# Moving the prompt's two key and value tiles behind the attention's first scores, and reloading weights in quarter pieces

## The chip, the cores and the metric

The kernel runs on one core of a Trainium2 chip. Its time is the device time of one execution in microseconds (us). Before the change the median of three runs is 1297.93 us (1297.85 to 1300.37).

## What is computed

The reference is one step of a two-layer backbone over 256 context ("prompt") tokens and 1024 latent ("sample") tokens of width 1024. Layer 0 is gated linear attention, layer 1 grouped-query softmax attention with 8 query heads and 2 key/value heads of size 128. The change lies in layer 1, at the seam between the output of layer 0 and the attention:

```
qp, kp, vp, gp = attn_project(hp, att_w_in, qnorm, knorm)      # prompt tokens
out_p = (attend_blocks(qp, kp, vp) * silu(gp)) @ att_w_out
ctx_keys.append(kp); ctx_vals.append(vp)                       # also outputs of the kernel
qs, ks_, vs, gs = attn_project(hs, att_w_in, qnorm, knorm)     # sample tokens
keys = concatenate([rope_2d(ks_), cache_k]); vals = concatenate([vs, cache_v])
out_s = (attend_blocks(rope_2d(qs), keys, vals) * silu(gs)) @ att_w_out
```

A sample query reads 1280 keys: the 1024 sample ones and 256 from a cache. Only the prompt's own queries read the prompt's keys and values.

## The kernel before

Every float32 product is made of three float16 ones: each factor is split into a high and a low part, and `mm3` (line 123) adds high by high, high by low and low by high. So one projection of 128 tokens to 512 columns is 24 matmuls of 512 columns, and one key and value tile, which reads its weights as two blocks of 256 columns (`pieces`, line 511), is 48 matmuls of 256 columns.

The tokens are cut into ten tiles of 128: 0 and 1 are the prompt, 2 to 9 the sample. `gla_out` (line 822) ends layer 0: it adds the residual, normalises, transposes, and makes the key and value tiles of all ten (`key_tile`, line 998), the sample's first and the prompt's last, by `keys(0)` on its last line, after the first two query projections. A key tile is a projection into a PSUM bank (tag "kv"), a copy to the tile `hx` on ScalarE (ACT), a norm of each head, a split of key and value into high and low, and a transposing DMA of the key into `kT` from the queue of SyncE (SP). For a prompt tile, ACT also writes the value into the only buffer of the tag "rope" (line 1012) and sends key and value to HBM.

`attention` (line 1141) then goes through ten steps, each a pair of a key head and a chunk of 256 tokens, four query heads to a step. The order of chunks is 1, 2, 3, 4, 0 for the first key head and 1, 0, 2, 3, 4 for the second; chunk 0 is the prompt, so steps 4 and 6 (counted from 0) are the prompt's. One head takes, for each of its two halves of 128 queries:

- `scores` (line 1043): 9 matmuls into S (three PSUM banks, two buffers), a maximum on VectorE (DVE, line 1059), an exponential on ACT (line 1064);
- `rest` (line 1070), held back by one half: the reciprocal, the division and split (line 1085 on GpSimd, POOL; line 1086 on DVE), and the transposing DMA to `PT` (line 1087, SP queue);
- two heads later `values` (line 1098): 30 matmuls on PT (6 for a prompt chunk).

Between the scores, `query` and `query_rest` make queries some steps ahead, and after each second head `gateT` (line 1090) makes two gates. The weights of these come from HBM: `load_w` (line 1113) calls `wload` (line 235), which with a list `later` puts its transfers there, and `attention` issues one from the list at each head. The query weights of the second key head ("q1") are listed at step 0, the gate weights ("g1") at step 4, the output weights ("o0") at step 6. Each lands in one of three places of SBUF; q1's place is the one that holds the first half of the key weights until the key tiles have read them.

The order written here is only a priority. A planner simulates the program when it is built and places each engine's instructions as soon as it believes them ready, so that a transfer can be issued well ahead of its line. On the chip each engine and each DMA queue then keeps the planned order.

Of the kernel before, what the change touches and what calls it, by code (L numbers as in the profile page):

```python
# [8 lines left out]
F32 = mybir.dt.float32  # L9
# [8 lines left out]
P = 128  # L18
D = 1024
KT = D // P  # L20
# [7 lines left out]
HD, AH, KVH = 128, 8, 2  # L28
# [28 lines left out]
class K:  # L57
# [126 lines left out]
    def fill(self, w, j, st):  # L184
        nc = self.nc
        s, w[2][j] = self.scale(st)
        h = KT // 4
        for i in range(4):
            a, n = slice(i * h, i * h + h), slice(256 * j, 256 * j + 256)
            hi, lo = w[0][:, a, n], w[1][:, a, n]  # L190
            nc.scalar.activation(hi, st[:, a, :], AF.Copy, scale=s)
            nc.vector.scalar_tensor_tensor(lo, st[:, a, :], s, hi, ALU.mult, ALU.subtract)
# [42 lines left out]
    def wload(self, name, place, later=None):  # L235
        d, inv = self.ahead.pop(name)
        w = self.wtile(place)[0:2]
        if later is None:
            for j, t in enumerate(w):
                self.nc.sync.dma_start(t, d[:, j])  # L240
        else:
            h = KT // 2
            later += [(t[:, a : a + h], d[:, j, a : a + h]) for j, t in enumerate(w) for a in (0, h)]
        return *w, inv


# [575 lines left out]
    def gla_out(self, wo, wkv):  # L822
        nc = self.nc
        done = len(EARLY)
        xs, junk = {}, self.t(self.xp, [P, D], F16, "junk", bufs=1)
        late = list(ROWS[done:])

        def fetch(i):
            xs[i] = self.t(self.xp, [P, D], F32, "xr", bufs=6)
            nc.sync.dma_start(xs[i], xrow(self.I, i) if i in late else self.x1_d[i])  # L830

        def norm(i):
            self.normalise([xs[i], xs[i + 1]], junk)

        def turn(i):
            ys = [xs.pop(i), xs.pop(i + 1)]
            for k in range(KT):
                self.modulate(self.transpose(ys, k, "tr"), k, i)

        def out(i):  # L840
            self.row_out(i, wo, xs[i])

        def keys(i):
            for j in range(2):
                self.key_tile(i + j, wkv)

        self.gs, self.sh, self.inv_h = self.mod1
        for i in (2, 3, 8, 4, 5, 9):
            fetch(i)
        d, inv = self.ahead.pop("kv")  # L850
        for j, w in enumerate(wkv):
            for part in range(2):
                nc.sync.dma_start(w[part], d[:, part, :, 256 * j : 256 * j + 256])
        ckv = self.att_load()
        self.o1 = []
        fill = self.out_part(2, self.kept2)
        norm(2)
        out(8)
        turn(2)
        norm(4)  # L860
        fetch(6)
        fetch(7)
        out(9)
        self.att_setup(*ckv)
        self.key_setup(*ckv, inv)
        self.wq = [self.load_w("q0", 2)]
        turn(4)
        fetch(0)
        fetch(1)
        fill(0)  # L870
        keys(2)
        norm(6)
        fill(1)
        out(0)
        fill = self.out_part(3, self.kept)
        turn(6)
        norm(8)
        keys(4)
        out(1)
        self.query_start()  # L880
        turn(8)
        fill(0)
        keys(6)
        norm(0)
        self.key_tile(8, wkv)
        self.query()
        turn(0)
        fill(1)
        self.key_tile(9, wkv)
        self.query_rest()  # L890
        self.query()
        self.query_rest()
        keys(0)

# [98 lines left out]
        nc.scalar.activation(self.vh[:, 8:10, :], cv, AF.Copy, scale=sv)  # L995
        nc.vector.scalar_tensor_tensor(self.vl[:, 8:10, :], cv, sv, self.vh[:, 8:10, :], ALU.mult, ALU.subtract)

    def key_tile(self, i, w):
        nc = self.nc
        j = i - NTP if i >= NTP else 10 + i  # L1000
        ps = self.bank("kv")
        self.pieces(ps, lambda k: self.hT(k, i * P, P), w, 0, 512)
        x = self.t(self.hw, [P, 2, HD], F32, "hx")
        nc.scalar.activation(x.rearrange("p h d -> p (h d)"), ps[:, 0:256], AF.Copy, scale=self.inv_k)
        self.head_norm(x, self.kn, x)
        pv = ps[:, 256:512]
        nc.scalar.activation(self.vh[:, j, :], pv, AF.Copy, scale=self.psv)
        nc.vector.scalar_tensor_tensor(self.vl[:, j, :], pv, self.psv, self.vh[:, j, :], ALU.mult, ALU.subtract)
        if i < NTP:
            nc.scalar.dma_start(self.O[3][0, 0, i * P : i * P + P], x)  # L1010
            v = self.t(self.hw, [P, 2, HD], F32, "rope", bufs=1)
            nc.scalar.activation(v.rearrange("p h d -> p (h d)"), pv, AF.Copy, scale=self.inv_av)
            nc.scalar.dma_start(self.O[4][0, 0, i * P : i * P + P], v)
        else:
            self.rope(x, i)
        a = slice(j * P, j * P + P)
        self.split_transpose(x, self.asc[:, 1:2], self.kT[:, :, a])
# [119 lines left out]
    def query_rest(self):  # L1137
        if self.half:
            self.queries_out(self.half.pop(), 1)

    def attention(self, wo):
        self.S0, self.put_off = self.t(self.ps, [P, 1536], F32, "S"), None
        wq, wg, q, g = self.wq, self.wg, self.q, {}
        pend, later = [], []
        for n, (p, c) in enumerate(self.steps):
            if n == 0:
                wq.append(self.load_w("q1", 1, later))
            if n == 4:
                wg.append(self.load_w("g1", 2, later))
            if n == 6:  # L1150
                o0 = self.wload("o0", 0, later)
            for e in range(4):
                h = 4 * p + e
                if later:
                    self.nc.sync.dma_start(*later.pop(0))
                PT = self.t(self.sp, [P, 20, 256], F16, "PT", bufs=3)
                self.scores(h, c, 0, q[(p, c, 0)], PT)
                if e % 2 == 0:
                    self.query()
                    self.scores(h, c, 1, q[(p, c, 1)], PT)  # L1160
                else:
                    self.query_rest()
                if len(pend) == 2:
                    self.values(*pend[0], g.pop(pend.pop(0)[0]))
                if e % 2 == 1:
                    self.scores(h, c, 1, q[(p, c, 1)], PT)
                pend.append((h, c, PT))
                if e % 2 == 1:
                    g.update({i: self.gateT(i, c, *wg[p]) for i in (h - 1, h)})
                if n == 9 and e == 0:  # L1170
                    row = self.out2_load(OUT[0])
                if n == 9 and e == 1:
                    first = self.ropet.rearrange("p a b d -> p (a b d)").bitcast(F16)
                    first = first.rearrange("p (j h t) -> p j h t", j=2, h=AH)
                    with self.tc.issue_after(self.last):
                        self.prep = self.out2_prep(row, (first[:, 0], first[:, 1]))
        self.rest()
        gt = self.t(self.wst, [P, KT, 256], F32, "wst").rearrange("p (i k) n -> p i (k n)", i=2)
        self.fold_gate(1, o0[2] + [inv for _, inv in self.o1], gt)
        wo[:] = [(*o0[0:2], 512)] + [(*w, 256) for w, _ in self.o1]  # L1180
        self.out_tile(OUT[0], 0, self.t(self.sp, [P, TS + PAST], F32, "p")[:, 0:D], wo)
        for t in pend:
            self.values(*t, g.pop(t[0]))
# [289 lines left out]
def xrow(I, i):  # L1473
    if i < NTP:
        return I["x_prompt"][0, i * P : i * P + P, :]
    return I["x_sample"][0, (i - NTP) * P : (i - NTP) * P + P, :]
# [84 lines left out]
```

## Time and profile before

| | |
|---|---|
| median of 3 runs | 1297.93 us |
| profiled execution | 1297.29 us |
| its span, first to last instruction | 1295.5 us |
| TensorE (PE) matmul busy | 1212.2 us, 94% |
| VectorE busy | 898.9 us, 69% |
| ScalarE busy | 581.4 us, 45% |
| GpSimd busy | 384.2 us, 30% |
| 16 DMA engines, mean rate | 150 GB/s |

The span plus 1.8 us around it is the profiled execution's time. PE is TensorE's matmuls, and a row's length for a matmul includes the pipeline's tail, so the distance from one start to the next tells what a matmul costs. In the timeline a bracket gives the idle time of the engine before the row and what released it. PEclk is the granted clock of TensorE: 1.00 is its upper level of 2.4 GHz, 0.50 the lower one of 1.2 GHz.

### The profile page before, as it was taken

The page shows a single profiled execution, that of the slowest core. Times are in us where ns is not written, and L with a number is a line of the kernel's source. Part 1 is how long each engine was busy: PE and PEld are TensorE (multiplying, and loading weights), DVE is VectorE, ACT ScalarE, POOL GpSimd, SP SyncE. Part 2 cuts the span into 40 slices and gives each one's busy share as a digit, 9 for nine tenths or more (in the row PEclk, how much of TensorE's full clock was granted, in tenths as well). Part 3 has the DMA queues.
Part 4 walks back from the last instruction along what each step waited for, and adds up shares of the span by engine and source line. Part 5 has one row for each costly group of instructions (what it writes and reads, how often), then busy time and mean ns, then how long its engine had stood idle before and what let it go on. Part 6 is the DMA issues. An engine that isn't in the chain of part 4 may idle for free. (4 is left out here: it accounts for less than half of the span.)

```text
span 1295.5 us, 22611 instructions
## 1 busy us (share of the span) xinstructions
PE 1212.2 (94%) x8295; PEld 811.9 (63%) x8295; DVE 898.9 (69%) x2072; ACT 581.4 (45%) x1425; POOL 384.2 (30%) x617
## 2 busy tenths in 40 slices
PE   4799989999998998999899989999999999989997
PEld 2347666655555555666688756667666766767665
DVE  5545866776688988755597667877657587885652
ACT  3445555555466665411265554444445455441110
POOL 0222211322232334400044535453233345522000
PEclk9899999999999999999999999999999999999999
DMA  9511454563443434995953357767848648778542
GB/s 359 191 65 34 146 180 124 157 193 103 150 117 119 126 114 158 283 199 141 326 161 101 81 116 140 135 130 147 191 94 172 146 86 144 145 143 197 174 131 82
DMA packets 333793, 194.42 MB, mean 150 GB/s; under 512 B 229663, under 2 KB 318607, under 8 KB 332401
## 3 DMA queue, kind: packets, MB, share of 16 engines
q1 hardware_dynamic: 291616, 159.02, 49.0%
q10 hardware_dynamic: 42064, 33.95, 8.4%
q8 instruction: 65, 1.06, 0.4%
q14 instruction: 48, 0.39, 0.1%
HBM read 103.00 MB, written 33.83 MB: 106 GB/s over the span
## 5 line engine op out<-in xcount | busy, mean ns | idle before, releaser
L131 PEld LDWEIGHTS <-hT_hi 128*128 128x128 f16 x1920 | 188.0, 98 | 126.9 <-issue 14.0
L131 PE MATMUL mm<-whi,hT_hi 128*128 128x512 f16 (+1 forms) x560 | 196.5, 351 | 6.5 <-ACT gx L535 5.6
L131 PE MATMUL mm<-wlo,hT_hi 128*128 128x512 f16 (+1 forms) x560 | 196.6, 351 | 0.0
L131 PE MATMUL mm<-whi,hT_lo 128*128 128x512 f16 (+1 forms) x560 | 196.6, 351 | 0.0
L131 PEld LDWEIGHTS <-whi 128*128 128x128 f16 x1408 | 138.0, 98 | 62.1 <-issue 9.2
L131 PE MATMUL mm<-hT_hi,whi 128*128 128x256 f16 (+1 forms) x512 | 153.3, 301 | 3.6 <-POOL hT_hi L410 2.9
L1085 POOL TENSOR_SCALAR phl<-p,srec 128x1280 f16<-128x1280 f32 (+1 forms) x80 | 98.8, 1235 | 188.2 <-DVE srec L1080 105.0
L131 PE MATMUL mm<-hT_lo,whi 128*128 128x256 f16 (+1 forms) x512 | 153.6, 301 | 0.2 <-DVE hT_lo L411 0.2
L131 PE MATMUL mm<-hT_hi,wlo 128*128 128x256 f16 (+1 forms) x512 | 153.7, 301 | 0.0
L1086 DVE SCALAR_TENSOR_TENSOR phl<-p,srec,phl 128x1280 f16<-128x1280 f32 (+1 forms) x80 | 107.7, 1347 | 51.6 <-POOL phl L1085 51.3
L131 PEld LDWEIGHTS <-hT_lo 128*128 128x128 f16 x960 | 94.2, 98 | 61.7 <-issue 1.0
L1056 PE MATMUL S<-kT,wst 128*128 128x512 f16 (+1 forms) x624 | 122.9, 341 | 7.5 <-ACT p L1064 7.1
L131 PE MATMUL mm<-PT,vh 128*128 128x256 f16 x672 | 114.3, 275 | 10.9 <-DMA PT<-phl 8.5
L1064 ACT ACTIVATE p<-S,snb,sexp 128x1280 f32<-128x1280 f32 (+1 forms) x80 | 99.7, 1246 | 29.4 <-DVE phl L1086 10.2
L1059 DVE TENSOR_REDUCE smx<-S 128x1 f32<-128x1280 f32 (+1 forms) x80 | 101.6, 1270 | 15.1 <-PE S L1056 15.1
L1056 PEld LDWEIGHTS <-wst 128*128 128x128 f16 x624 | 61.4, 98 | 60.4 <-issue 10.2
L131 PE MATMUL mm<-PT,vl 128*128 128x256 f16 x336 | 92.4, 275 | 0.0
L131 PEld LDWEIGHTS <-wlo 128*128 128x128 f16 x704 | 69.0, 98 | 29.5 <-issue 1.4
L1061 ACT ACTIVATE snb<-smx,nsexp 128x1 f32<-128x1 f32 x80 | 23.4, 293 | 131.9 <-DVE smx L1059 126.6
L131 PEld LDWEIGHTS <-vh 128*128 128x128 f16 x672 | 65.8, 99 | 21.9 <-issue 10.0
L917 POOL TENSOR_TENSOR rope<-hx,ropet 128x64 f32<-128x64 f32 x160 | 69.9, 465 | 10.3 <-DVE hx L906 4.7
L153 DVE TENSOR_REDUCE wmx<-wst 128x1 f32<-128x512 f32 x96 | 59.8, 676 | 11.8 <-DMA wst<-in_gla_w_in 10.4
(347 smaller groups left out, 2494.7 us busy)
## 6 DMA issues: line engine op xcount, KB each, us to landing
wada<-in_w_ada SPq DMA_DIRECT2D x13, 1024.0 KB
wst<-in_gla_w_in SPq DMA_DIRECT2D x12, 1024.0 KB
wst<-in_att_w_in SPq DMA_DIRECT2D x10, 1024.0 KB
xr<-x_d SPq DMA_DIRECT2D x15, 512.0 KB
og_d<-qk ACTq DMA_DIRECT2D x40, 128.0 KB
wst<-og_d SPq DMA_DIRECT2D x5, 1024.0 KB
out<-xr ACTq DMA_DIRECT2D x17, 256.0 KB
x<-in_x_sample SPq DMA_DIRECT2D x8, 512.0 KB
```

Of the source, the lines that this page charges most:

```text
L131: self.nc.tensor.matmul(out, a, b, start=k == 0 and j == 0, stop=k == n - 1 and j == 2)
L153: nc.vector.tensor_reduce(mx[:, j : j + 1], st[:, 2 * j : 2 * j + 2, :], AX.XY, ALU.max, apply_absolute_value=True)
L917: nc.gpsimd.tensor_tensor(tv[:, h, :, w, :], xv[:, h, :, 1 - w, :], sn[:, :, w, :], ALU.mult)
L1056: nc.tensor.matmul(S[:, a : a + n], x, y, start=m == 0, stop=m == 2)
L1059: last = nc.vector.tensor_reduce(mx, S, AX.X, ALU.max).ins
L1061: nc.scalar.activation(nb, mx, AF.Copy, scale=self.nsexp)
L1064: nc.scalar.activation(p, S, AF.Exp, scale=self.sexp, bias=nb, accum_out=den)
L1085: nc.gpsimd.tensor_scalar(hi, p, r, 2.0 ** 14, ALU.mult, ALU.mult)
L1086: nc.vector.scalar_tensor_tensor(lo, p, r2, hi, ALU.mult, ALU.subtract)
```

## The change

The two prompt tiles leave the end of `gla_out`. Their weights are held, the second half is loaded again (its first copy lies in a pool that ends with `gla_out`) beside the first, and each tile is made in `attention` behind the first scores of heads 0 and 1 of step 0. There it uses the PSUM tag "mm" and the tile tag "hx4", both shared with the queries. The listed weight loads come as eight transfers of 256 KB in place of four of 512 KB, in order of use; q1 is listed at step 1, o0 at step 7, and g1 at step 4 from its second head on, two transfers a head, the last two at the first head of step 5.

```diff
         else:
-            h = KT // 2
-            later += [(t[:, a : a + h], d[:, j, a : a + h]) for j, t in enumerate(w) for a in (0, h)]
+            h = KT // 4
+            later += [(t[:, a : a + h], d[:, j, a : a + h]) for a in range(0, KT, h) for j, t in enumerate(w)]
...
-        keys(0)
+        self.held_keys = d, wkv
...
-    def key_tile(self, i, w):
+    def key_tile(self, i, w, tag="kv"):
...
-        ps = self.bank("kv")
+        ps = self.bank(tag)
...
-        x = self.t(self.hw, [P, 2, HD], F32, "hx")
+        x = self.t(self.hw, [P, 4, HD], F32, "hx4")[:, 0:2] if tag == "mm" else self.t(self.hw, [P, 2, HD], F32, "hx")
...
+    def prompt_keys(self):
+        d, wkv = self.held_keys
+        hi, lo, _ = wkv[0]
+        again = [t[:, :, 0:256] for t in self.nw[0:2]]
+        for part, t in enumerate(again):
+            self.nc.sync.dma_start(t, d[:, part, :, 256:512])
+        w = [wkv[0], (*again, 256)]
+        return lambda i: self.key_tile(i, w, "mm")
...
             if n == 0:
+                keys = self.prompt_keys()
+            if n == 1:
                 wq.append(self.load_w("q1", 1, later))
             if n == 4:
                 wg.append(self.load_w("g1", 2, later))
-            if n == 6:
+            if n == 7:
                 o0 = self.wload("o0", 0, later)
             for e in range(4):
                 h = 4 * p + e
-                if later:
-                    self.nc.sync.dma_start(*later.pop(0))
+                for _ in range((0, 2, 2, 2)[e] if n == 4 else 2 if n == 5 else 1):
+                    if later:
+                        self.nc.sync.dma_start(*later.pop(0))
                 PT = self.t(self.sp, [P, 20, 256], F16, "PT", bufs=3)
                 self.scores(h, c, 0, q[(p, c, 0)], PT)
+                if n == 0 and e < 2:
+                    keys(e)
```

## Rows read from the trace of the kernel before

**Rows 1.** The page, busy time and the span in 40 slices, PE and its clock.
```profile
PE 1212.2 (94%) x8295; PEld 811.9 (63%) x8295; DVE 898.9 (69%) x2072; ACT 581.4 (45%) x1425; POOL 384.2 (30%) x617
...
PE   4799989999998998999899989999999999989997
...
PEclk9899999999999999999999999999999999999999
```

**Rows 2.** Timeline of PE at the seam: start, duration, work, idle before and releaser.
```profile
729.79 0.27 PE L131 MATMUL kv<-whi,hT_hi 128*128 128x256 f16 x1
...
740.73 1.79 PE L1056 MATMUL S<-kT,wst 128*128 128x512 f16 x9
742.35 0.38 PE L131 MATMUL mm<-whi,hT_hi 128*128 128x512 f16 x1
...
747.32 0.38 PE L131 MATMUL mm<-whi,hT_lo 128*128 128x512 f16 x1
748.08 1.78 PE L1056 MATMUL S<-kT,wst 128*128 128x512 f16 x9 [0.39 <-ACT rope L1012]
753.28 3.15 PE L1056 MATMUL S<-kT,wst 128*128 128x512 f16 x9 [3.42 <-ACT p L1064]
756.27 0.27 PE L131 MATMUL mm<-hT_hi,whi 128*128 128x256 f16 x1
```

**Rows 3.** Timeline of ACT and DVE, the first softmax and what stands before it.
```profile
747.56 0.47 ACT L1012 ACTIVATE rope<-kv,inv_av 128x256 f32<-128x256 f32 x1 [2.51 <-DMA out<-rope]
749.48 0.48 DVE L934 SCALAR_TENSOR_TENSOR xhl<-hx,asc,xhl 128x256 f16<-128x256 f32 x1 [2.80 <-ACT xhl L933]
749.88 1.48 DVE L1059 TENSOR_REDUCE smx<-S 128x1 f32<-128x1280 f32 x1
751.73 1.42 ACT L1064 ACTIVATE p<-S,snb,sexp 128x1280 f32<-128x1280 f32 x1
```

**Rows 4.** Timeline of SP's queue: the last transposes and q1's four transfers.
```profile
732.33 1.19 SPq L935 DMA_TRANSPOSE kT<-xhl  x1
735.32 1.19 SPq L935 DMA_TRANSPOSE wst<-xhl  x1
736.60 1.00 SPq L1155 DMA_DIRECT2D wlo<-w_q  x2
739.64 1.20 SPq L935 DMA_TRANSPOSE wst<-xhl  x1
740.94 1.00 SPq L1155 DMA_DIRECT2D whi<-w_q  x2
```

**Rows 5.** Busy us by engine (instructions), PE clock, DMA share, GB/s, in stretches of 1 us.
```profile
734.00:735.00 1.00, 1.00 (x11) 0.80 (x10) 1.00 (x5) 0.72 (x4) 0.29 (x1) 1.00 0.16 32
735.00:736.00 1.00, 1.00 (x11) 0.90 (x10) 0.86 (x4) 0.39 (x2) 0.84 (x2) 1.00 0.00 0
740.00:741.00 1.00, 1.00 (x11) 0.80 (x9) 0.86 (x3) 0.06 (x1) 0.07 (x1) 1.00 0.94 360
754.00:755.00 1.00, 1.00 (x4) 0.35 (x3) 0.28 (x2) 0.94 (x6) 0.03 (x1) 0.50 0.00 0
```

**Rows 6.** Timeline of PE and ACT, the rest of step 0: waits, and its eighth exponential.
```profile
778.38 1.78 PE L1056 MATMUL S<-kT,wst 128*128 128x512 f16 x9 [1.77 <-ACT p L1064]
781.56 0.39 PE L131 MATMUL mm<-PT,vh 128*128 128x256 f16 x2 [1.40 <-DMA PT<-phl]
786.04 1.42 ACT L1064 ACTIVATE p<-S,snb,sexp 128x1280 f32<-128x1280 f32 x1 [1.14 <-DVE srec L1080]
```

**Rows 7.** Timeline of SP's queue and of PE, step 4 (prompt chunk) and g1's transfers.
```profile
917.24 1.01 SPq L1155 DMA_DIRECT2D whi<-w_g  x2
926.08 1.04 SPq L1155 DMA_DIRECT2D wlo<-w_g  x2
...
936.68 0.38 PE L131 MATMUL mm<-PT,vh 128*128 128x256 f16 x2
939.96 0.71 PE L1056 MATMUL S<-kT,wst 128*128 128x256 f16 x5
943.35 0.38 PE L131 MATMUL mm<-PT,vh 128*128 128x256 f16 x2 [2.69 <-DMA PT<-phl]
948.29 0.27 PE L1056 MATMUL S<-kT,wst 128*128 128x256 f16 x1
```

**Rows 8.** Busy us by engine, clock, DMA share: g1's load, then two full stretches.
```profile
925.00:930.00 5.00, 5.00 (x47) 4.33 (x45) 3.69 (x6) 2.17 (x4) 1.33 (x1) 1.00 0.97 226
930.00:935.00 5.00, 5.00 (x33) 2.94 (x31) 2.50 (x9) 1.61 (x5) 0.00 (x0) 1.00 1.16 224
800.00:850.00 50.00, 50.00 (x360) 35.05 (x359) 38.89 (x71) 23.32 (x55) 25.89 (x31) 1.00 0.68 127
```

**Rows 9.** Timeline of PE: the other wait that a load may touch, and o0's first use.
```profile
1000.20 0.38 PE L131 MATMUL mm<-PT,vh 128*128 128x256 f16 x2 [1.82 <-DMA PT<-phl]
...
1172.74 0.38 PE L131 MATMUL S<-whi,ropet 128*128 128x512 f16 x1
```

## The prediction

> **What bounds the kernel now.** I read the page first: PE is busy for 94% of the span, and apart from the first slices every slice is nearly full and the clock is at its upper level [rows 1]. No engine other than PE comes near. So the time falls only where PE stands or runs at the lower clock, and moved work gains only where it fills such a place. Next I listed PE's waits from the seam between the layers to the end of the attention; they sit at the seam and in the rest of step 0, in the prompt steps, and late in the second key head, where the change does nothing. Between, in the stretch from 800 to 850 us, PE is busy for all 50.00 us [rows 8].
>
> At the seam PE works without a gap until 747.5 us: the two prompt tiles from 729.79 to 740.73 us, the first S, a query of 24 matmuls, then a second S after 0.39 us. The third S needs a free buffer, that is the first S's exponential, and PE stands for 3.42 us [rows 2]. Why is that exponential late? The first S is complete at about 742.5 us, but its maximum starts only at 749.88 us. DVE and ACT hold the second prompt tile ahead of it: ACT's copy at 747.56 us had idled 2.51 us for the output DMA that still read the one "rope" buffer, and DVE idled 2.80 us behind ACT [rows 3]. The clock follows: after the wait it is granted at 0.50, the level of 1.2 GHz [rows 5], and the nine matmuls of the third S take 2.99 us from start to next start (753.28 to 756.27) where the first took 1.62 us (740.73 to 742.35) [rows 2].
>
> **The change, part by part.**
>
> *The prompt tiles move.* Nothing leaves PE: 96 matmuls of 256 columns before and after. They ran for 10.94 us (729.79 to 740.73, a few transposes among them) ahead of the first S [rows 2]. What did the first S wait for otherwise? The last sample key was issued to its transpose at 732.33 us [rows 4], and the DMA engines are at rest by 735 us [rows 5]. So the first S can start at about 735 us, 5.5 us earlier. PE need not stand from 730 to 735 us: the first prompt tile (half of 10.94, 5.5 us) and a query (742.35 to about 747.5, 5.2 us) are ready, and the planner may place either first. Without the prompt's vector work ahead, maximum and exponential follow at once: from the maximum's start to the exponential's end takes 3.27 us (749.88 to 751.73 plus 1.42) [rows 3]. The first buffer is then free at about 735.2 + 1.8 + 3.3 = 740.3 us. PE's way to the third S is 10.94 (tile and query, 5.5 + 5.2, rounded) + two S of 1.62 from 729.8 us, so it comes there at 743.7 us or later and finds the buffer free. The second S's 0.39 us goes with the release by the copy of line 1012, which no longer holds its bank. Gain: 0.39 + 3.42 + the lower clock's 2.99 - 1.62 = 1.37, sum 5.2 us. I take all of it; the bounds are 0 (the hold returns inside the step) and 5.2.
>
> *The rest of step 0.* The eight exponentials start 4.90 us apart on average (751.73 to 786.04, seven intervals) [rows 3, 6]. PE offers less in the first two heads: four S of 1.62, a query of 5.2, two gates of half a query each, 16.9 us or 4.2 us a half. So it catches up with the chain and stands 1.77 us for an exponential and 1.40 us for a transposed PT [rows 6]. With 10.94 us more it needs 7.0 us a half there, over 4.90, and the wait for the exponential should go: 1.8 us. The wait for PT I leave, because q1's load moves onto the first PT transposes (next part). Bounds 0 and 3.2.
>
> *The second half of the key weights is loaded again:* two transfers of 512 KB more on SP's queue. Two such issues take 1.00 us of the queue [rows 4]; at the 360 GB/s of a stretch that holds only such loads [rows 5] 1.05 MB takes 2.9 us. Lower bound 0, upper 3.9 if the planner puts them right ahead of the last key's transpose. I take 0, because PE has the 10.7 us of tile and query to do while the first S waits; without that cover the first S slips by as much.
>
> *Twelve more issues,* three loads of eight in place of four: at 0.5 us of SP's queue each [rows 4], spread one or two to a head. A transpose queued behind two waits about 1 us more; values come two heads later, over 10 us. Cost 0. If SP were already late, up to 1 us a head.
>
> *q1 moves to step 1.* It now waits until both prompt tiles have read their weights, so it comes at about 745 to 755 us or later instead of 736.60 to 742 us [rows 4]. It then lies beside PT transposes rather than ahead of them. Its 2.1 MB need 5.8 us of all engines at 360 GB/s [rows 5]. In full steps, at a DMA share of 0.68 with PE never waiting [rows 8], it costs 0; at most those 5.8 us if all of it falls before the first PT. I take 0 beyond the 1.40 us that I left standing.
>
> *g1.* Before, its four transfers leave at 917.24 and 926.08 us [rows 7] and fill the DMA engines up to about 937 us (shares 0.97 and 1.16 [rows 8]). The PT transposes behind them are late: PE waits 2.69 us at 943.35 us, and then at the lower clock its 30 matmuls take 4.94 us (943.35 to 948.29) against 3.28 us for the same number just before (936.68 to 939.96) [rows 7]; 2.69 + 1.66 = 4.35 us in all. The change starts the load one head later, and puts at most 512 KB between two heads' transposes. But the queue may be planned ahead of its lines, so part of the load can still lie where it did. Bounds 0 and 4.35; I take half, 2.2 us, because about half the bytes are still issued in the second and third heads.
>
> Here a rule of the Trainium skill speaks against the change. What the rows show is that transfers of 512 KB run at 360 GB/s back to back [rows 5], with no visible gap between them. "DMA: Bandwidth & Descriptors", section "Rules for kernel authors", asks for at least 1 MiB a transfer for full bandwidth. By the sizes in its table "Measured" a straight line gives, as an estimate, 2.0 us for 256 KB and 3.4 us for 512 KB, so 16 us for a load in eight pieces and 13.5 us in four; by that g1's gain would be lost and the sum would be 7.0 us.
>
> *o0 moves to step 7.* Its first use is at 1172.74 us [rows 9], far behind; cost 0. It frees the start of step 5, so the 1.82 us at 1000.20 us [rows 9] could shrink; I take 0, upper bound 1.8.
>
> **Sum.** 5.2 + 1.8 + 2.2 = 9.2 us off the profiled execution's 1297.3, which is 1288.1. The median of the runs shown is 0.6 us above that execution, so 1288.7.
>
> **The rivals.**
>
> *A. The prompt step's wait stays.* The planner issues g1 as early as before, or the small pieces keep the engines as full. For it: in the trace transfers run well ahead of their lines, and the load's bytes are the same. Against it: g1's wait has transposes stuck behind pairs of 512 KB. Only the seam gains: 1297.9 - 7.0 = 1290.9, or 1292.7 if the wait for the exponential stays too.
>
> The rule of the Trainium skill named above leads to this case.
>
> *B. All of it comes.* 5.2 + 3.2 + 4.35 + 1.8 = 14.5 us: 1283.4. For it: each of these waits has its cause among the transfers and the work moved. Against it: every term at its bound.
>
> *C. The hold returns inside step 0: no change.* A prompt tile still needs the one "rope" buffer, now shared with the queries' rotation, and ACT must wait at line 1012 as it did for 2.51 us [rows 3], with exponentials queued behind it. Two tiles, each holding ACT for 2.5 to 5 us, give back the 5.2 us; the change does not do what it moves the work for. Against it: PE then has 10.94 us more to cover. Time 1297.
>
> *D. Slower: q1 runs into the first PT transposes.* If its whole 5.8 us lies ahead of the first head's PT, the wait at 781.56 us grows from 1.40 to 7.2 us and the lower clock follows it, as it did after 2.69 us, for 1.66 us: 7.5 us more against the seam's 5.2, so 2.3 us net, and with SP's twelve more issues (0.5 us each for the eight of this load, 4 us) up to 6 us. Time about 1301. It decides as soon as the first PT lands more than 5 us later than now relative to PE. For it: the load cannot start until the prompt tiles are done. Against it: it is listed at one piece a head.
>
> **How the numbers follow.** A measurement of this kernel can tell about 0.2%, 2.6 us, from no change. Chances: the forecast 0.45 (own range 1286 to 1290.5), A 0.25, B 0.08, C 0.12, D 0.10. Faster by more than 0.2%: forecast, A and B, 0.78. Within: C, 0.12. Slower: D, 0.10. The range from 1284.0 to 1298.5 leaves out D and most of B, less than 0.2.
>
> **What would show it.** Right: the first S at about 735 us, maximum right behind it, the third S without a wait for the exponential, no clock of 0.50 near 754 us, PE with no longer wait at the first PT, and a shorter wait in step 4. Wrong: the first S still behind a prompt tile with its maximum late; ACT idle ahead of line 1012 inside step 0; SP's queue with a run of q1's pieces ahead of the first PT transposes; or a new wait of PE for gate weights early in step 5, where g1's last pieces are due.

## The result, and the profile after

The change makes the kernel slower: 1302.67 us (median of 12 runs, 1298.92 to 1305.84) against 1296.16 us of the kernel before (12 runs, 1291.08 to 1300.37). The ratio is 1.0057, with a 95% interval of 1.0044 to 1.0070; the medians are 6.5 us apart. The forecast was 1288.7, faster.

PE's waits in the changed kernel, from its timeline, with the same columns as before:

```profile
733.35 0.81 PE L1056 MATMUL S<-kT,wst 128*128 128x512 f16 x3 [3.01 <-ACT h L409]
736.39 1.14 PE L1056 MATMUL S<-kT,wst 128*128 128x512 f16 x6
...
745.38 3.41 PE L1056 MATMUL S<-kT,wst 128*128 128x512 f16 x18
...
762.14 2.00 PE L1056 MATMUL S<-kT,wst 128*128 128x256 f16 x11
...
782.89 0.58 PE L131 MATMUL mm<-PT,vh 128*128 128x256 f16 x2 [6.82 <-DMA PT<-phl]
790.29 1.79 PE L1056 MATMUL S<-kT,wst 128*128 128x512 f16 x9
...
933.67 0.82 PE L1056 MATMUL S<-kT,wst 128*128 128x256 f16 x6
948.08 0.59 PE L131 MATMUL mm<-PT,vh 128*128 128x256 f16 x2 [4.01 <-DMA PT<-phl]
972.26 1.79 PE L1056 MATMUL S<-kT,wst 128*128 128x512 f16 x9
```

The first S has a new stop of 3.01 us. The waits for an exponential at the seam and in the rest of step 0 are gone, as are the stops of [rows 2] and the first one of [rows 6]. The row at 762.14 us holds the last two matmuls of the fifth S and the nine of the sixth, which starts at 762.35 us. In the kernel before the sixth starts at 769.93 us, behind a query of 5.2 us that the changed kernel has still to do, so PE is about 2.4 us ahead here. Then 6.82 us go at once. Step 1's first S is at 790.29 us, 2.8 us later than before. In step 4 the wait of 2.69 us [rows 7] has become 4.01 us, and the lead of the old kernel grows again: step 5 begins at 972.26 us, 5.6 us later than before. Nearly the whole loss is made by then. The two starts in the kernel before:

```profile
787.47 1.79 PE L1056 MATMUL S<-kT,wst 128*128 128x512 f16 x9
...
966.68 1.79 PE L1056 MATMUL S<-kT,wst 128*128 128x512 f16 x9
```

What filled SP's queue ahead of those two waits? Its timeline, in step 0 and before step 4:

```profile
765.47 3.75 SPq L1087 DMA_TRANSPOSE PT<-phl  x1
769.28 0.57 SPq L1167 DMA_DIRECT2D wlo<-w_q  x1
769.89 0.42 SPq L1167 DMA_DIRECT2D whi<-w_q  x1
770.41 1.20 SPq L935 DMA_TRANSPOSE kT<-xhl  x1
771.66 0.57 SPq L1167 DMA_DIRECT2D wlo<-w_q  x1
772.28 0.43 SPq L1167 DMA_DIRECT2D whi<-w_q  x1
772.75 0.43 SPq L1167 DMA_DIRECT2D wlo<-w_q  x1
773.23 0.54 SPq L1167 DMA_DIRECT2D whi<-w_q  x1
773.81 0.43 SPq L1167 DMA_DIRECT2D wlo<-w_q  x1
774.34 5.26 SPq L1087 DMA_TRANSPOSE PT<-phl  x1
...
928.01 0.57 SPq L1167 DMA_DIRECT2D whi<-w_g  x1
928.63 0.59 SPq L1167 DMA_DIRECT2D wlo<-w_g  x1
929.26 0.43 SPq L1167 DMA_DIRECT2D whi<-w_g  x1
929.74 0.43 SPq L1167 DMA_DIRECT2D wlo<-w_g  x1
930.21 0.43 SPq L1167 DMA_DIRECT2D whi<-w_g  x1
930.69 1.50 SPq L1167 DMA_DIRECT2D wlo<-w_g  x1
932.28 18.84 SPq L1087 DMA_TRANSPOSE PT<-phl  x5
```

The source lists q1 at one piece a head over steps 1 and 2. The planner put all eight into step 0, seven of them in a run (with one key transpose among them) between the second head's two PT transposes; the second is issued at 774.34 us, and PE gets it at 782.89 us. Its input was complete at 770.52 us. The source starts g1 one head later; the planner issued its first two pieces at 919.93 us and the other six from 928.01 us, as early as before (917.24 and 926.08 [rows 7]), and now six in a run right ahead of five transposes. The busy time by engine around the first run (the last three columns are PE clock, DMA share and GB/s) shows the price twice:

```profile
776.00:780.00 4.00, 0.07 (x1) 0.00 (x0) 3.79 (x7) 1.36 (x2) 0.67 (x3) 0.90 1.13 264
780.00:784.00 4.00, 1.11 (x6) 0.81 (x7) 0.55 (x3) 0.94 (x4) 1.06 (x1) 0.50 1.26 225
784.00:788.00 4.00, 4.00 (x29) 3.14 (x28) 2.60 (x5) 1.51 (x2) 4.00 (x6) 0.75 0.61 116
```

PE is idle for most of 776 to 783 us while the DMA engines are full, and it runs on at 0.50, the level of 1.2 GHz, into the third stretch.

### The profile page after: what moved, and what is told of

Read it like the earlier page. It is cut to its first block, busy times and chain, and to the rows that moved or that the text cites. A ratio compares the mean times of both kernels' runs of the same rounds, so it can differ in the third digit from the quotient of the medians.

```text
span 1300.3 us, 22624 instructions
## 1 busy us (share of the span) xinstructions
PE 1215.0 (93%) x8295; PEld 812.5 (62%) x8295; DVE 898.7 (69%) x2072; ACT 580.3 (45%) x1425; POOL 386.6 (30%) x617
## 3 DMA queue, kind: packets, MB, share of 16 engines
q8 instruction: 65, 1.06, 0.3%
## 5 line engine op out<-in xcount | busy, mean ns | idle before, releaser
L131 PE MATMUL mm<-whi,hT_hi 128*128 128x512 f16 (+1 forms) x592 | 205.2, 347 | 7.4 <-ACT gx L535 6.5
L131 PE MATMUL mm<-whi,hT_lo 128*128 128x512 f16 (+1 forms) x592 | 205.4, 347 | 0.0
L131 PE MATMUL mm<-wlo,hT_hi 128*128 128x512 f16 (+1 forms) x592 | 205.3, 347 | 0.0
```

Source lines behind the costliest of these rows:

```text
L131: self.nc.tensor.matmul(out, a, b, start=k == 0 and j == 0, stop=k == n - 1 and j == 2)
```

## The experiments

A theory and two rivals. **T**: the loss is the place of the loads. q1 and g1 go out as runs ahead of PT transposes, whatever the size of a piece. The rivals: the moved tiles' work on ACT, DVE and POOL makes the softmax chain late (R); small pieces are slow in themselves (S).

Single spans can't be compared here, since the stage before the seam alone shifts them (one 0.32 us stop of a key tile lies at 675.32 us in the changed kernel's profile and at 679.03 us in that of the other-banks kernel below, where the code differs in a bank order only). So besides the ratio I use two stretches of each profile that hold nearly the same PE work: from the start of the seam's last transposing matmul (line 398) to the first S of step 4, and from there to the first S of step 5, both worked out from starts of matmuls in the trace. In the kernels that move the tiles the first stretch holds five more matmuls of 256 columns, about 0.5 us, which the others run ahead of its start. Each stretch comes from one profile, in which the lower clock may have followed a stop or not; that alone can make 1.7 us (see the last section).

All kernels are timed against the kernel before, in four sets: the changed kernel; tiles only to other banks; all tied to all tied, query first; and the last three. The kernel before had medians of 1296.16, 1296.49, 1295.80 and 1295.84 us in them, and each ratio is to its own set. So ratios, not medians, compare rows of different sets.

| kernel | median us | ratio to before, 95% interval | seam to step 4 | step 4 |
|---|---|---|---|---|
| before | 1296.16 | 1 | 200.2 | 35.8 |
| changed | 1302.67 | 1.0057 (1.0044 to 1.0070) | 203.6 | 38.6 |
| tiles only | 1299.41 | 1.0022 (1.0005 to 1.0039) | 206.8 | 33.5 |
| loads only | 1297.02 | 0.9997 (0.9981 to 1.0013) | 198.8 | 37.2 |
| q1 tied | 1295.33 | 0.9996 (0.9983 to 1.0009) | 195.9 | 37.0 |
| other banks | 1301.61 | 1.0043 (1.0029 to 1.0058) | 204.6 | 38.6 |
| all tied | 1291.47 | 0.9949 (0.9925 to 0.9972) | 197.5 | 31.3 |
| all tied, 512 KB | 1291.43 | 0.9958 (0.9937 to 0.9980) | 197.0 | 31.3 |
| before, g1 tied | 1292.83 | 0.9971 (0.9951 to 0.9990) | 200.4 | 32.1 |
| all tied, query first | 1293.81 | 0.9976 (0.9956 to 0.9996) | 200.6 | 31.3 |
| all tied, tile first | 1288.78 | 0.9950 (0.9937 to 0.9963) | 197.0 | 31.3 |
| before, q1 as a run | 1297.69 | 1.0019 (1.0005 to 1.0033) | 202.9 | 33.7 |
| loads only, tied | 1290.57 | 0.9969 (0.9951 to 0.9987) | 198.4 | 31.3 |

**Tiles only.** The loads of the change are taken back:

```diff
-            h = KT // 4
+            h = KT // 2
-            ... for a in range(0, KT, h) for j, t in enumerate(w)]
+            ... for j, t in enumerate(w) for a in (0, h)]
-            if n == 7:
+            if n == 6:
-                for _ in range((0, 2, 2, 2)[e] if n == 4 else 2 if n == 5 else 1):
+                for _ in range(1):
```

> The prompt tiles move as in the change, but all three loads stay in pieces of 512 KB in the old order and at one a head (q1 at step 1, g1 at step 4 from its first head, o0 at step 6). Theory T (the loss in step 0 is q1's load, planned as one run ahead of the second head's PT transposes, whatever the size of its pieces): the PT wait near 783 us stays at 5 us or more, and step 4 gets back to about the 2.7 us wait of before; total 2 to 5 us over the kernel before. Rival S (small pieces are slow): the PT wait falls under 2 us and the kernel is 2 us or more under before. Rival R (the tiles' vector work makes the softmax chain late): the wait stays at 6 to 7 us, as T.

From the timeline of PE:

```profile
785.02 0.58 PE L131 MATMUL mm<-PT,vh 128*128 128x256 f16 x2 [7.59 <-DMA PT<-phl]
948.94 0.38 PE L131 MATMUL mm<-PT,vh 128*128 128x256 f16 x2 [1.97 <-DMA PT<-phl]
```

As T has it: with pieces of 512 KB the wait in step 0 is 7.59 us, and step 4 is no worse than before. S falls for step 0. R is still open. The total, 1.0022, is in the range that T gave.

**Loads only.** The kernel before with the change's pieces and heads, the tiles at their old place and q1 at step 0.

```diff
-            h = KT // 2
+            h = KT // 4
-            if n == 6:
+            if n == 7:
+                for _ in range((0, 2, 2, 2)[e] if n == 4 else 2 if n == 5 else 1):
```

> The prompt tiles stay where they were; only the loads change (256 KB pieces; q1 at step 0 as before, g1 and o0 at the change's heads). T: the seam is as before (third S waits 3.4 us), step 0 as before, and step 4 carries the change's wait of about 4 us in place of 2.7 us, with a longer stretch at the lower clock: 1 to 3 us over before. Rival S: 3 us or more over before, spread over all three loads. If the g1 part of the forecast held: 2 us under before.

```profile
752.43 1.78 PE L1056 MATMUL S<-kT,wst 128*128 128x512 f16 x9 [1.82 <-ACT p L1064]
943.83 0.59 PE L131 MATMUL mm<-PT,vh 128*128 128x256 f16 x2 [3.91 <-DMA PT<-phl]
```

Step 4 has the changed kernel's wait, 3.91 us, without the tiles, so that part belongs to g1's load as it was changed. But the total is not over before, because the seam was not as before: the third S waits 1.82 us in place of 3.42 [rows 2]. So part of the seam's old loss hung on q1's load, not on the tiles' place.

**q1 tied.** The changed kernel, with each piece of q1 made to follow, in SP's queue, the PT transpose before it in the source:

```diff
-        nc.sync.dma_start_transpose(PT[...], parts)
+        self.last_T = nc.sync.dma_start_transpose(PT[...], parts).ins
...
+                    if later and n < 4:
+                        with self.tc.issue_after(self.last_T):
+                            self.nc.sync.dma_start(*later.pop(0))
```

> The changed kernel, with each of q1's pieces tied behind the PT transpose that stands before it in program order, so that it goes out at one a head in steps 1 and 2; nothing else moves. T: the 6.8 us PT wait of step 0 falls to 2.5 us or less (the transpose's own time behind its phl), the lower clock after it mostly goes, and the kernel is 4 to 6 us under the changed one. Rival R: the wait stays at 5 us or more and the time within 2 us of the changed kernel.

From the timeline of PE, with the second head's second PT transpose from SP's (the second row):

```profile
731.97 0.81 PE L1056 MATMUL S<-kT,wst 128*128 128x512 f16 x3 [2.29 <-ACT h L409]
769.53 3.73 SPq L1087 DMA_TRANSPOSE PT<-phl  x1
774.64 0.38 PE L131 MATMUL mm<-PT,vh 128*128 128x256 f16 x2 [0.49 <-DMA PT<-phl]
938.98 0.38 PE L131 MATMUL mm<-PT,vh 128*128 128x256 f16 x2 [3.87 <-DMA PT<-phl]
```

6.82 us became 0.49 us with the tiles where the change put them. R falls: their work is still all there, and the transpose that PE waits for has its input hardly earlier. From the last transposing matmul of the seam the input takes 40.1 us here and 40.5 us in the changed kernel. Here it is issued at once (769.53 us) and used 5.1 us later; there it is issued 3.8 us after its input and used 8.6 us later. The run delays it in both ways, on the queue and on its way. Seam to step 4 is 7.7 us shorter than in the changed kernel, more than I expected, and step 4 keeps its 3.87 us.

**Other banks.** This asks what the new stop of 3.01 us at the first S is.

```diff
-            k.held = {t: k.bank(t) for t in ("y", "tr", "kv", "mm")}
+            k.held = {t: k.bank(t) for t in ("y", "kv", "tr", "mm")}
```

> The changed kernel, with the PSUM banks of the stage before the attention handed out in the order y, kv, tr, mm in place of y, tr, kv, mm, so that the first S does not take over a bank of the transposes that feed the prompt tiles; order and count of instructions stay. If the 3.0 us stop of PE at the first S is that bank's release: it goes, and the first S starts at about 730.4 us; total 3 us under the changed kernel, unless the softmax chain and PT eat it (then the PT wait of step 0 grows by as much, and the total stays). If the stop is something else (the key transposes): it stays.

```profile
735.21 0.82 PE L1056 MATMUL S<-kT,wst 128*128 128x512 f16 x3
739.06 0.28 PE L131 MATMUL mm<-whi,hT_hi 128*128 128x256 f16 x1 [1.06 <-POOL hT_hi L410]
740.20 0.28 PE L131 MATMUL mm<-whi,hT_lo 128*128 128x256 f16 x1 [0.75 <-DVE hT_lo L411]
```

The stop was the bank's release: the first S now follows the last transposes. But PE then stands 1.06 and 0.75 us for the prompt tile's own input, and nothing is gained (204.6 against 203.6 us): with the PT wait of 6.40 us the three stops are 1.6 us shorter than the changed kernel's two, but the clock is granted at 0.50 from 742 to 744 us, behind the new ones, which it was not behind the 3.01 us. In both orders the planner put in front of PE what was not ready.

**All tied.** The tie of q1 for all three loads (no `n < 4`).

> The changed kernel with every piece of q1, g1 and o0 tied behind the PT transpose that stands before it in program order. T (a planned run of pieces ahead of PT transposes costs the time; the change's own heads would do): step 0 as with q1 alone tied (PT wait 0.5 us), and in step 4 the wait of 3.9 us falls under 1 us with no clock of 0.50 after it; 4 to 6 us under the kernel before, 10 us under the changed one. Rival G (g1 tied is too late for the gates of step 5): a new wait of PE for weights near 975 us of 2 us or more, and no gain over q1 tied alone. Rival N (the step 4 wait is the softmax chain's, not the load's): the wait stays at 2 us or more.

SP's timeline around step 4, with the pieces between the transposes:

```profile
937.86 0.57 SPq L1168 DMA_DIRECT2D whi<-w_g  x1
938.48 0.42 SPq L1168 DMA_DIRECT2D wlo<-w_g  x1
941.76 1.20 SPq L1087 DMA_TRANSPOSE PT<-phl  x1
943.06 3.25 SPq L935 DMA_TRANSPOSE wst<-xhl  x2
946.42 1.21 SPq L1087 DMA_TRANSPOSE PT<-phl  x1
947.67 0.57 SPq L1168 DMA_DIRECT2D whi<-w_g  x1
```

Step 4 has no wait of PE left: 31.3 us in place of 38.6, and the gates of step 5 wait for nothing. This kernel beats both, the old one by its ratio of 0.9949.

**All tied, 512 KB.** The same heads, half as many pieces (`h = KT // 2`, one a head).

> As the kernel with every piece tied, but in pieces of 512 KB (one a head; g1 from the second head of step 4 to the first of step 5): the same bytes behind the same heads, only the size of a piece differs. If the size of a piece matters as the skill's rule has it (bigger is faster): 1 us or more under the tied quarter pieces. If small pieces help by letting transposes in between: 1 us or more over them, with a PT wait of 1 us or more in step 4. T: the same within 1 us, since where the run lies is what counts.

1291.43 against 1291.47 us, and the same 31.3 us in step 4. With its place fixed, the size of a piece made no difference that these runs show; the rule of the Trainium skill that I weighed ("DMA: Bandwidth & Descriptors", section "Rules for kernel authors": at least 1 MiB a transfer) decided nothing here either way; both sizes lie below it.

**Before, g1 tied.** The tie at `n == 4` alone, in the kernel before.

> The kernel before with one edit: g1's four transfers of 512 KB are tied behind the PT transpose that stands before each at its head of step 4. It measures the forecast's g1 term by itself. T: the 2.7 us wait at 943 us and the lower clock after it go; 3 to 4.5 us under the kernel before. Rival N: the wait stays at 2 us or more and the time within 1 us of before.

```profile
938.52 0.38 PE L131 MATMUL mm<-PT,vh 128*128 128x256 f16 x2 [0.60 <-DMA PT<-phl]
```

2.69 us became 0.60, and step 4 is 3.7 us shorter (35.8 to 32.1): the forecast's g1 term was there to be had, by tying four transfers.

**Before, q1 as a run.** This puts q1's load of the old kernel where the changed kernel has it: the four transfers are held to the third head of step 0 and tied as one run behind the second head's first PT transpose.

```diff
+                if n == 0 and e == 2:
+                    with self.tc.issue_after(self.last_T):
+                        while later:
+                            self.nc.sync.dma_start(*later.pop(0))
```

> The kernel before with one edit: q1's four transfers of 512 KB are held to the third head of step 0 and go out as one run between the second head's two PT transposes, where the changed kernel has them; the prompt tiles stay. T: this alone makes the loss: a PT wait of PE in step 0 of 5 us or more with the clock at 0.50 after it, and 3 to 7 us over the kernel before. Rival R (the moved tiles' work is needed for it): the PT wait stays under 3 us and the time within 2 us of before.

From the timelines of ACT (the first row) and PE:

```profile
746.03 0.47 ACT L1012 ACTIVATE rope<-kv,inv_av 128x256 f32<-128x256 f32 x1 [0.35 <-DMA out<-rope]
751.74 1.78 PE L1056 MATMUL S<-kT,wst 128*128 128x512 f16 x9 [0.27 <-ACT p L1064]
781.57 2.65 PE L1056 MATMUL S<-kT,wst 128*128 128x512 f16 x9 [3.85 <-ACT p L1064]
784.95 0.61 PE L131 MATMUL mm<-PT,vh 128*128 128x256 f16 x2 [0.73 <-DMA PT<-phl]
```

Half a hit. It is slower without the moved tiles, and the lower clock follows, but by 1.0019 and not by the 3 us or more that I named, and PE stands for an exponential where I had written PT. The planner here put that S, step 1's first, ahead of the second head's values. Their PT was issued at 776.01 us and used at 784.95 us, 8.9 us later, as in the changed kernel (8.6) and not as with q1 tied (5.1); in the time before it PE stands for 3.85 and 0.73 us. So the run holds the transpose up without the moved tiles too. The row at 751.74 us tells why the total is small: with q1's load gone from the seam the third S waits 0.27 us in place of 3.42, with the prompt tiles still ahead of the first S. So the run cost more than the total shows.

**Loads only, tied.** The loads-only kernel with g1 and o0 tied.

> The loads of the change with g1's and o0's pieces tied behind PT transposes, the prompt tiles at their old place and q1 at step 0 as before. Against the kernel with every piece tied it gives what the move of the tiles is worth by itself. Forecast's seam term less the new stop at the first S: 5.2 + 1.8 - 2.3, so this kernel is 4 to 5 us over the tied one and about 2 to 4 us under the kernel before. If the move is worth nothing: the two are the same.

0.9969 against 0.9949 for all tied, 2.6 us, and the intervals overlap; seam to step 4 is 198.4 against 197.5 us, 1.4 us at equal work. The move of the tiles by itself is worth about 1.4 to 2.6 us here, less than the 4 to 5 that I expected, and these runs don't show it apart from zero.

**Query first, tile first.** Two ways to fill the stop at the first S in the all-tied kernel: the step's first query, or the first prompt tile, ahead of the first scores.

> As the kernel with every piece tied, and the first query of step 0 stands ahead of the first scores. If the stop of PE at the first S (2.3 to 3.0 us) is only uncovered waiting for a bank and hT: 24 matmuls of 5.2 us cover it, it goes, and the kernel is 2 to 3 us under the one with every piece tied. If the softmax chain sets step 0: the first S is later by as much, a wait for an exponential or PT of 2 us or more appears in step 0, and the time stays.

> As the kernel with every piece tied, and the first prompt tile stands ahead of the first scores, the second behind those of head 1. If the stop of PE at the first S (2.3 to 3.0 us) is uncovered waiting: about 20 matmuls of the tile (2.2 us) cover it, the first S is not later (its last matmuls wait for the last sample key anyway), the stop falls under 1 us and the kernel is 1 to 2.5 us under the one with every piece tied. If the chain sets step 0: a wait for an exponential of 2 us or more appears, and the time stays.

```profile
758.89 1.68 PE L1056 MATMUL S<-kT,wst 128*128 128x512 f16 x6 [3.46 <-ACT p L1064]
```

```profile
733.28 0.28 PE L131 MATMUL mm<-whi,hT_hi 128*128 128x256 f16 x1 [1.80 <-POOL hT_hi L410]
```

With the query first PE waits 3.46 us for an exponential (the first row): the chain sets step 0, and nothing is won. With the tile first the stop stays at 1.80 us (the second row), for the tile's own input, where I had expected less than 1 us. Its median of six runs, 1288.78 us, is the lowest of all, but its ratio of 0.9950 is that of all tied.

## Why the prediction was wrong

*The seam.* The mechanism held: the third S no longer waits, nor does the eighth, and the clock near 754 us is granted at 1.00. The size did not. 5.2 + 1.8 = 7.0 us were forecast from the seam and step 0; with q1 tied the stretch to step 4 is 4.3 us under before, with all tied 2.7 (4.8 and 3.2 at equal work; the second profile has the lower clock behind the stop at the first S, the first has not). The step that failed is "PE need not stand from 730 to 735 us". The planner put the first three matmuls of the first S there, and they stand 2.3 to 3.0 us for a bank. And the 3.42 us were put down to the prompt tiles; the runs with q1 elsewhere or in smaller pieces (0.27 and 1.82 us, tiles in place) show that q1's load made a large part of them. The traces show by what path: the first output from "rope", issued at 742.12 us, holds the buffer to 747.56 us in the kernel before, 5.4 us, and ACT waits 2.51 us for it [rows 3]; with smaller pieces it is 4.4 us, and with q1 elsewhere 2.9 us (743.18 to 746.03) and a wait of 0.35. That the output is slow because it shares the DMA engines with q1's load is argued, not shown. Of the 5.2 us, 1.37 were the lower clock behind that wait, and the last section shows that it need not follow.

*q1.* "I take 0 beyond the 1.40 us" was the costliest term. The wait measured 6.82 us, with the lower clock after it, and tying q1 shortens the stretch by 7.7 us. I had written that transfers run well ahead of their lines, and still priced q1 by its lines. Rival D named this mechanism, and about its time (1301); its place was the second head's PT, not the first's, and it took seven of the eight pieces. That its time came so near is partly luck: it counted the seam's 5.2 us in full and nothing for step 4.

*g1.* "I take half, 2.2 us" failed in its sign. Counted from the first S of step 4, the load began as early as before (13.7 us ahead against 13.6), and its second part earlier (5.7 against 4.8). Only the half megabyte that the first pair no longer held went out later, and it joined the run: that grew from two transfers of 512 KB to six of 256 KB, and step 4 took 2.8 us more (35.8 to 38.6). My upper bound of 4.35 us was about right for what an actual delay gives: 3.7 us in the old kernel, 4.5 us with all tied.

*The rest.* The second load of the key weights and twelve more issues cost nothing that the tied kernels show; nor did o0. Rival C did not come: ACT does not wait for the shared "rope" buffer in the changed kernel. The rule of the Trainium skill that led to rival A played no part.

*The sum.* Seam to step 4 +3.4 us (2.9 at equal work), step 4 +2.8 us: 6.2 us in the profiles, against 6.5 us between the medians.

## What to carry to other kernels

Where a planner orders the queues, a transfer moved in the source need not have moved: look up where its issue stands in the queue, and tie it behind the work that it must not overtake. A transfer that nobody waits for can still be the costliest one, if a run of it stands ahead of a small transfer that the bottleneck needs next. And before a stall is put down to the work beside it, ask what else moved in that stretch: moving that alone may give most of it back.

## What was not expected of the hardware

The lower clock does not follow the length of a wait by itself. The kernel before with g1 tied has the old seam, with the same wait of 3.42 us at the third S. In the kernel before the clock after it is granted at 0.50 [rows 5], and the nine matmuls take 2.99 us; here it is granted at 1.00, and they take 1.62 us (750.54 to 752.16). The first row is the third S, the second the busy time by engine, then clock, DMA share and GB/s:

```profile
750.54 1.78 PE L1056 MATMUL S<-kT,wst 128*128 128x512 f16 x9 [3.42 <-ACT p L1064]
```

```profile
751.00:753.00 2.00, 2.00 (x16) 1.42 (x15) 1.02 (x2) 1.72 (x9) 0.70 (x1) 1.00 0.00 0
```

Another pair: the same stop in the last step, 2.06 us in the kernel before (up to 1145.86 us), was followed by a granted clock of 1.00; 2.07 us in the all-tied kernel (up to 1140.61 us) by 0.50. The first row is of before, the second of all tied:

```profile
1146.00:1148.00 2.00, 2.00 (x20) 1.79 (x19) 2.00 (x2) 0.23 (x2) 1.21 (x1) 1.00 1.14 216
```

```profile
1142.00:1144.00 2.00, 2.00 (x12) 1.41 (x10) 2.00 (x2) 0.00 (x0) 0.00 (x0) 0.50 0.85 160
```

The price of a short stop therefore varies: nothing beyond the stop, or, in the all-tied kernel, about 1.7 us more (an estimate from the clock of 0.67, 0.50 and 0.98 in the three stretches of 2 us from 1140 us on). What decides it, these runs don't show.
